# Two residual gates and a norm vector: spread over the partitions by one product with the partial sums, or read broadcast from DRAM

## The chip, the cores and the metric

The kernel runs on one NeuronCore of a Trainium2 chip. The metric is the device time of one execution in microseconds (us). The engines are named as in the profile: PE (TensorE), PEld (its weight loads), DVE (VectorE), ACT (ScalarE), POOL (GpSimd), SP (SyncE, which here only issues DMAs; SPq is its queue).

## The reference, cut to what matters

One layer: a mixing sub-layer (RWKV-7 and a causal convolution, merged by gates) and a squared-ReLU MLP, each added to the residual through a gate that depends on a vector `c`. 512 tokens, 1024 channels, all in float32.

```
mod = silu(c) @ ada_w + ada_b                       # 6 segments of 1024
sh_m, sc_m, gt_m, sh_f, sc_f, gt_f = split(mod, 6)
...
x = x + gt_m * (merged @ w_out)                     # merged: 512 x 2048
h = rms_norm(x, norm_ffn_gain) * (1 + sc_f) + sh_f
x = x + gt_f * (square(relu(h @ w_ff_in)) @ w_ff_out)
return rms_norm(x, final_gain)
```

The change touches `gt_m` (segment 2), `gt_f` (segment 5) and `final_gain`. Each is one value for a channel, and tokens lie on the partitions where they are used, so each must stand in all 128 partitions: a 128x1024 tile.

## The kernel before, in words

Every large product is done in three passes of two fp32r parts: a weight tile `raw` is loaded by DMA, ACT casts it to `hi`, DVE or POOL subtracts to give `lo`, and PE runs hi·high, hi·low, lo·high. The names are `raw_wo`, `hi_wo`, `lo_wo` for the output product and `raw_fi`, `hi_fi`, `lo_fi` for the first MLP product.

The middle of the kernel is a list of steps, written out by hand in `ORDER`: R, I, V, O, M, S, Y are the RWKV part, U and T the convolution, G and B the merging gates (`ga`, `gb`), L reloads merged tiles that were spilled (`mr`), W is one step of the output product, A half a segment of `mod`, Q the spread of the first gate. The number behind a colon is a priority offset: the tile framework's scheduler sorts the instructions of each engine by priority and by when their operands are free, so the order in the program text is not the order on the engines. Every engine then works in its own order and waits where an operand is missing. All weight, `ada_w` and reload DMAs stand in one order on SP.

After the last RWKV group `enter_tail` opens the pools of the tail (near 606 us). What runs from there to 735 us:

- **A steps.** `mod_half` loads eight 128x512 tiles `ar` of `ada_w` (256 KB each, three buffers) and sums them on DVE, each weighted by a column of `silu(c)`, in `aacc`: partial sums that still have to be added over the 128 partitions. `mod_cols` does that with four products with a column of ones (`pmv`, 128x1) and adds the bias (`ab`) into `modt`: one value for a channel, channels on the partitions. There are eight A steps, A0 to A7, for segments 2 to 5: 0 and 1 give gate `gt_m` (`modt[0]`), 2 and 3 `sh_f` (`modt[1]`), 4 and 5 `sc_f` (`modt[2]`), 6 and 7 `gt_f` (`modt[3]`). In the list their order is A3, A0, A5, A7, A1, A6, Q, A2, A4.
- **W steps.** The product of `merged` with `w_out`, in two halves of 512 columns, each 16 row tiles, accumulated over all 16 for four token tiles (`acc_wo`, four PSUM buffers). `wo_out` multiplies by the gate (`t_wo`) and adds to the residual `x`. In the second half the last seven row tiles (`WLATE`) are kept back and run token tile by token tile.
- **h2.** After the last row tile, `h2_norm` for each of the four token tiles (square on ACT, a chain of some ten 128x1 operations on DVE in `srow`, then `xn`) and `h2_tile` (PE transposes `ph`, then scale `modt[2]` and shift `modt[1]` into `hf` on ACT and DVE, and the parts `hh`, `hl`). The first four column tiles of the MLP (`ps_fi`, `ff_part`) run on token tiles 0 and 1 first (128x256 moving), then on 2 and 3.

`spread` is how a gate gets to all partitions: DVE makes a diagonal matrix `dg` from a column of `modt`, PE multiplies ones by it (128x128, float32, two records each), eight times for one gate, and ACT copies 512 columns out of PSUM twice. It runs three times: for `gate_t` in step Q, and for `gate_f` and `fgain` in the MLP, both after its fifth column tile.

Of the kernel before, what the change touches and what calls it, by code (L numbers as in the profile page):

```python
# [8 lines left out]
F32 = mybir.dt.float32  # L9
# [3 lines left out]
ALU = mybir.AluOpType  # L13
# [28 lines left out]
)  # L42
WLATE = 9
# [19 lines left out]
def tile_rwkv7_conformer(  # L63
# [19 lines left out]
    ident = const.tile([P, P], F32, name="ident")  # L83
# [79 lines left out]
    def mm3(ps, w, m):  # L163

        for k in range(KT):
            last = mm3k(ps, w, m, k)
        return last
# [55 lines left out]
            PE.matmul(pm[:, i:i + 1], acc[:, i * P:(i + 1) * P], ones[:, 0:1], start=True, stop=True)  # L223
        V.tensor_tensor(dst[:, 4 * h:4 * h + 4], pm, ab[:, 8 * seg + 4 * h:8 * seg + 4 * h + 4], op=ALU.add)

    def spread(pool, psp, tag, dst, col, nm):

        for h in range(2):
            pb = psp.tile([P, 512], F32, tag=tag, name=f"psp_{nm}{h}")
            for i in range(4):  # L230
                dg = pool.tile([P, P], F32, tag="dg", name=f"dg_{nm}{h}{i}", bufs=2)
                V.tensor_scalar(dg, ident, col[:, 4 * h + i:4 * h + i + 1], None, op0=ALU.mult)
                PE.matmul(pb[:, i * P:(i + 1) * P], ones, dg, start=True, stop=True)
            S.copy(dst[:, 512 * h:512 * h + 512], pb)

    def wrow(src, r0, h, nm, eng=None, own=None):
        raw = wp.tile([P, 512], F32, tag="wraw", name=f"raw_{nm}")
# [9 lines left out]
    with tc.tile_pool(name="e1", bufs=1) as e1, tc.tile_pool(name="e2", bufs=2) as e2:  # L247
# [184 lines left out]
        for n, ap, k in [(n, ap, 8) for n, ap in (  # L432
                ("a0", a0[0]), ("k_k", k_k[0]), ("k_a", k_a[0]), ("r_k", rk_flat), ("gn_gain", gn_gain[0]),
                ("gn_bias", gn_bias[0]), ("conv_b", conv_b[0]), ("ln_gain", conv_ln_gain[0]),
                ("ln_bias", conv_ln_bias[0]), ("nfg", norm_ffn_gain[0]), ("fgain", final_gain))] + [("mu", mu_shift[0], 26)]:
            nc.sync.dma_start(out=rows[1][r:r + k, :], in_=ap.rearrange("(t p) -> t p", p=P))
            VEC[n] = vt[:, r:r + k]
            r += k
        nc.sync.dma_start(out=rows[2], in_=cwr[72:200])
        nc.sync.dma_start(out=rows[3][0:48, :], in_=cwr[200:248])  # L440
        for i, (dst, n0) in enumerate(((vt, 114), (cw[:, 72:200], 128), (cw[:, 200:248], 48))):
            pt = pq.tile([P, 512], F32, tag="m", name=f"ptv{i}", bufs=2)
            PE.transpose(pt[:, 0:n0], rows[i + 1][0:n0, :], ident[0:n0, 0:n0])
            V.tensor_copy(dst, pt[:, 0:n0])
# [8 lines left out]
    with ExitStack() as c1:  # L453
# [368 lines left out]
        def enter_tail():  # L822

            cq.close()
            m2 = c1.enter_context(tc.tile_pool(name="m2", bufs=1, reuse_waits="tile"))
            p2 = ctx.enter_context(tc.tile_pool(name="p2", bufs=1, space=PSUM, reuse_waits="tile"))
            tail["ct"] = c1.enter_context(ExitStack())
            tpool[0] = tail["ct"].enter_context(tc.tile_pool(name="t2", bufs=1, reuse_waits="tile"))
            tail["m2"], tail["p2"] = m2, p2
            tail["mh"], tail["ml"] = {}, {}  # L830
            x1.extend(tok_halves("x1_"))
            gate.append(m2.tile([P, D], F32, tag="gt", name="gate_t"))
            for i in range(2):
                nc.sync.dma_start(out=x1[i], in_=x2d.rearrange("(h t p) n -> h p t n", p=P, t=2)[i])

# [113 lines left out]
        def step(op):  # L949
            k, i = op[0], int(op[1:] or 0)  # L950
            if k == "R":
                quarters.setdefault(i // 2, []).append(rkv_pair(i))
            elif k == "I":
                scans[i] = products(i, quarters[i])
            elif k == "V":
                scans[i] = solve(i, scans[i])
            elif k == "O":
                scans["o", i] = scan_operands(i, quarters[i])
            elif k == "M":
                scans[i] = merge_inverses(i, *scans[i])  # L960
            elif k == "S":
                RT, RVs = scans[i], scans["o", i]
                scans[i] = scan(i, quarters[i], RVs, RT)
            elif k == "Y":
                group_norm(i, quarters[i], *scans[i])
                if i == 3:
                    enter_tail()
            elif k == "U":
                scans["gl", i] = conv_tile(i)
            elif k == "T":  # L970
                conv_taps(i, scans.pop(("gl", i)))
            elif k == "G":
                gate_a(i)
            elif k == "N":
                scans["cn"] = conv_norm()
            elif k == "B":
                gate_b(i, *scans["cn"])
            elif k == "L":
                reload()
            elif k == "A":  # L980
                seg, h = 2 + i // 2, i % 2
                acc = mod_half(modt[seg - 2], seg, h, V)
                mod_cols(pp, "o", modt[seg - 2], acc, seg, h)
            elif k == "Q":
                spread(tail["m2"], tail["p2"], "m", gate[0], modt[0], "gm")
            elif k == "W":
                wo_step(int(wn[0] == 16))

# [5 lines left out]

    p2 = tail["p2"]
    with tc.tile_pool(name="s3", bufs=2, reuse_waits="tile") as s3:
        gate_f = s3.tile([P, D], F32, name="gate_f", bufs=1)
        fgain = s3.tile([P, D], F32, name="fgain", bufs=1)
        ssum = s3.tile([P, NT, 6], F32, name="ssum", bufs=1)

        def ff_rows(acc, n, k, wh, wl, fh, fl, tt):
# [40 lines left out]
        for fq in range(NFQ):  # L1042
            fh = s3.tile([P, KT, T], F32R, tag="fh", name=f"fh{fq}")
            fl = s3.tile([P, KT, T], F32R, tag="fl", name=f"fl{fq}")
            for i in range(KT):
                if fq == 0 and i < NFF:
                    ps = first_ff[i]
                else:
                    w = wcol(w_ff_in[0], fq * D + i * P, f"fi{fq}{i}", G if fq == 0 and GFI > i else None)
                    ps = pp.tile([P, T], F32, tag="pp", name=f"ps_fi{fq}{i}", bufs=2)  # L1050
                    mm_last = mm3(ps, w, (hh, hl))
                f = s3.tile([P, T], F32, tag="f", name=f"f{fq}{i}")
                S.activation(f, ps, AF.Relu)
                V.tensor_tensor(f, f, f, op=ALU.mult)
                S.copy(fh[:, i, :], f)
                V.tensor_tensor(fl[:, i, :], f, fh[:, i, :].bitcast(F32), op=ALU.subtract)
                if fq == 0 and i == max(SPR, NFF):
                    with tc.issue_after(mm_last.ins):
                        spread(s3, p2, "m", gate_f, modt[3], "gf")
                        spread(s3, p2, "m", fgain, VEC["fgain"], "fg")  # L1060
            last = fq == NFQ - 1
            for h in range(2):
                acc = [p2.tile([P, 512], F32, tag="acc", name=f"acc_fo{fq}{h}{tt}", bufs=4) for tt in range(NT)]
                held = []
                for k in range(KT):
                    own = (s3, "late", KT - FLATE) if last and h == 1 and k >= FLATE else None
                    with ahead(LHP if own else 0):
                        wh, wl = wrow(w_ff_out[0], fq * D + P * k, h, f"fo{fq}{h}{k}", None, own)
                    if own:
                        held.append((k, wh, wl))  # L1070
                        continue
                    for tt in range(NT):
                        ff_rows(acc, k, k, wh, wl, fh, fl, tt)
                for tt in range(NT):
                    for k, wh, wl in held:
                        ff_rows(acc, k, k, wh, wl, fh, fl, tt)
                    if last and h == 1:
# [32 lines left out]
```

## Time and profile before

| what | value |
|---|---|
| time, three runs | 1129.80 us median (1123.34 to 1132.21) |
| the profiled execution | 1131.94 us, span 1130.2 us |
| mean granted clock of TensorE | 0.953 of full speed |
| PE busy | 1023.5 us (91%) |
| DVE busy | 790.1 us (70%) |
| ACT busy | 479.1 us (42%) |
| POOL busy | 198.2 us (18%) |
| DMA | 131.34 MB, mean 116 GB/s |

The profile is of one execution; its times start at the first instruction. PE's busy time is modelled at the ends of matmuls, so the distance from one start to the next says more than the duration. "[1.38 <-DVE xn L905]" behind a row means that the engine had been idle 1.38 us and that line 905 on DVE released it.

### The profile page before, as it was taken

How to read it: one execution, taken by the hardware profiler on the slowest of the kernel's cores; microseconds unless marked ns; L12 is line 12 of the kernel's file. 1: busy time of each engine (PE TensorE's matmuls, PEld its weight loads, DVE VectorE, ACT ScalarE, POOL GpSimd, SP SyncE). 2: the span in 40 equal slices, each digit the busy share in tenths (PEclk: the TensorE clock that was granted, in tenths of full speed). 3: DMA queues.
4: the chain of work that ended last, by engine and by line, in shares of the span. 5: the costliest groups of instructions: out<-in, count | busy, mean ns of one | idle time of the engine just before them, and what ended most of it. 6: DMA issues, size and time to landing. Idle time of an engine off the chain costs nothing.

```text
span 1130.2 us, 16757 instructions
## 1 busy us (share of the span) xinstructions
PE 1023.5 (91%) x6037; PEld 792.5 (70%) x6037; DVE 790.1 (70%) x1622; ACT 479.1 (42%) x912; POOL 198.2 (18%) x191
## 2 busy tenths in 40 slices
PE   2999889889899789996997999899999999999995
PEld 1777666656677666665665767688888888888874
DVE  3859999969958997989455787585445445445557
ACT  5546445374644356534343433264323323423432
POOL 1123042222422533221121121200000000000002
PEclk9999999989999989996798999999999999999998
DMA  9622332331343234324257686731223323333332
GB/s 313 181 72 87 88 100 73 54 92 48 104 117 94 86 95 83 85 66 110 94 162 234 224 273 217 232 104 38 84 93 95 101 94 94 95 93 100 96 103 74
DMA packets 184605, 131.34 MB, mean 116 GB/s; under 512 B 49945, under 2 KB 152779, under 8 KB 184523
## 3 DMA queue, kind: packets, MB, share of 16 engines
q1 hardware_dynamic: 184523, 130.28, 39.1%
q8 instruction: 47, 0.77, 0.3%
q14 instruction: 35, 0.29, 0.1%
HBM read 116.61 MB, written 13.63 MB: 115 GB/s over the span
## 4 chain that ended last, share of the span: by engine, by line
PE 43%; DVE 16%; DMA 5%; issue 3%; ACT 3%; POOL 1%; SPq 0%; DVEq 0%; ACTq 0%; POOLq 0%
PE ps_fi L174 5%; PE ps_fi L175 5%; PE ps_fi L176 5%; DVE cz L745 5%; PE acc_fo L1005 4%; PE acc_fo L1004 4%; PE acc_fo L1003 4%; DMA ar<-in_ada_w_dram 2%; DVE tmp L598 1%; DVE aacc L217 1%; PE ps_ga L175 1%; PE ps_ga L176 1%; PE ps_ga L174 1%; DVE X L600 1%; PE pr L669 1%
## 5 line engine op out<-in xcount | busy, mean ns | idle before, releaser
L745 DVE SCALAR_TENSOR_TENSOR cz<-gl,cw,cz 128x512 f32<-128x512 f32 x240 | 200.8, 837 | 3.9 <-ACT cz L743 1.2
L151 DVE TENSOR_TENSOR lo_fo<-raw_fo,hi_fo 128x512 fp32r<-128x512 f32 x64 | 44.2, 691 | 92.1 <-ACT hi_fo L150 91.9
L175 PE MATMUL ps_fi<-hl,hi_fi 128*128 128x512 f32 (+1 forms) x288 | 105.6, 367 | 0.0
L176 PE MATMUL ps_fi<-hh,lo_fi 128*128 128x512 f32 (+1 forms) x288 | 105.3, 367 | 0.0
L174 PE MATMUL ps_fi<-hh,hi_fi 128*128 128x512 f32 (+1 forms) x288 | 105.0, 367 | 0.0
L1003 PE MATMUL acc_fo<-hi_fo,fh 128*128 128x512 f32 x256 | 101.3, 396 | 0.8 <-DVE t_fo L1010 0.8
L1004 PE MATMUL acc_fo<-lo_fo,fh 128*128 128x512 f32 x256 | 101.2, 395 | 0.0
L1005 PE MATMUL acc_fo<-hi_fo,fl 128*128 128x512 f32 x256 | 101.2, 395 | 0.0
L150 ACT CAST hi_fo<-raw_fo 128x512 fp32r<-128x512 f32 x64 | 39.7, 621 | 110.6 <-PE acc_fo L1005 87.8
L151 DVE TENSOR_TENSOR lo_fi<-raw_fi,hi_fi 128x512 fp32r<-128x512 f32 x64 | 43.8, 690 | 52.1 <-ACT hi_fi L150 51.2
L150 ACT CAST hi_fi<-raw_fi 128x512 fp32r<-128x512 f32 x64 | 39.9, 623 | 74.0 <-PE ps_fi L175 45.6
L1021 POOL TENSOR_TENSOR x<-x,fgain 128x512 f32<-128x512 f32 x4 | 5.5, 1392 | 363.8 <-ACT sq L1015 363.8
L175 PEld LDWEIGHTS ps_fi<-hl,hi_fi 128*128 128x128 f32 x288 | 54.3, 189 | 8.9 <-DVE hl L928 0.4
L176 PEld LDWEIGHTS ps_fi<-hh,lo_fi 128*128 128x128 f32 x288 | 54.3, 189 | 8.7
L174 PEld LDWEIGHTS ps_fi<-hh,hi_fi 128*128 128x128 f32 x288 | 54.0, 189 | 8.8 <-ACT hh L927 0.2
L174 PE MATMUL ps_u<-hh,hi_u 128*128 128x512 f32 x128 | 54.1, 422 | 5.4 <-DVE tr L466 2.9
L937 PE MATMUL acc_wo<-lo_wo,mh 128*128 128x512 f32 x128 | 53.0, 414 | 5.9 <-DVE lo_wo L151 3.2
L217 DVE SCALAR_TENSOR_TENSOR aacc<-ar,cact,aacc 128x512 f32<-128x512 f32 x56 | 49.9, 891 | 11.3 <-DMA ar<-in_ada_w_dram 10.7
L1003 PEld LDWEIGHTS acc_fo<-hi_fo,fh 128*128 128x128 f32 x256 | 48.2, 188 | 12.7 <-DVE t_fo L1010 1.3
L1005 PEld LDWEIGHTS acc_fo<-hi_fo,fl 128*128 128x128 f32 x256 | 48.2, 188 | 11.5
L1004 PEld LDWEIGHTS acc_fo<-lo_fo,fh 128*128 128x128 f32 x256 | 48.2, 188 | 11.5
L176 PE MATMUL ps_u<-hh,lo_u 128*128 128x512 f32 x128 | 54.9, 429 | 0.6 <-POOL Pt L512 0.6
(334 smaller groups left out, 2554.3 us busy)
## 6 DMA issues: line engine op xcount, KB each, us to landing
ar<-in_ada_w_dram SPq DMA_DIRECT2D x64, 256.0 KB
raw_fi<-in_w_ff_in_dram SPq DMA_DIRECT2D x64, 256.0 KB
raw_fo<-in_w_ff_out_dram SPq DMA_DIRECT2D x64, 256.0 KB
araw<-in_ada_w_dram SPq DMA_DIRECT2D x8, 1024.0 KB
raw_u<-in_w_in_dram SPq DMA_DIRECT2D x32, 256.0 KB
raw_wo<-in_w_out_dram SPq DMA_DIRECT2D x32, 256.0 KB
raw_k<-in_w_in_dram SPq DMA_DIRECT2D x16, 256.0 KB
raw_v<-in_w_in_dram SPq DMA_DIRECT2D x16, 256.0 KB
```

The costliest lines, as they stand in the source:

```text
L150: S.copy(hi, raw)
L151: (eng or V).tensor_tensor(lo, raw, hi.bitcast(F32), op=ALU.subtract)
L174: PE.matmul(ps[:, ts_], wh[:, i, :], mh[:, k, ts_], start=first, stop=False, skip_group_check=True)
L175: PE.matmul(ps[:, ts_], wh[:, i, :], ml[:, k, ts_], start=False, stop=False, skip_group_check=True)
L176: return PE.matmul(ps[:, ts_], wl[:, i, :], mh[:, k, ts_], start=False, stop=(k == KT - 1), skip_group_check=True)
L217: eng.scalar_tensor_tensor(acc, a, cact[:, k:k + 1], acc, op0=ALU.mult, op1=ALU.add)
L598: V.tensor_tensor(tv, X[:, 0:n, s:s + 1].to_broadcast([P, n, m]), U[:, s:s + 1, s + 1:32].to_broadcast([P, n, m]), op=ALU.mult)
L745: V.scalar_tensor_tensor(cz, gl[:, w:w + T], cw[:, w * KT + j:w * KT + j + 1], cz, op0=ALU.mult, op1=ALU.add)
L937: PE.matmul(wacc[h][tt], mh[k][:, ts_], wl, start=False, stop=False)
L1003: PE.matmul(acc[tt], fh[:, k, ts_], wh, start=(n == 0), stop=False)
L1004: PE.matmul(acc[tt], fh[:, k, ts_], wl, start=False, stop=False)
L1005: PE.matmul(acc[tt], fl[:, k, ts_], wh, start=False, stop=(n == KT - 1))
```

## The change

For segments 2 and 5, `mod_cols` is replaced by `gate_half`: one product of a 128x128 matrix of ones with the 128x512 partial sums puts their sum over the partitions into every partition of a PSUM tile (`pgt`), and one DVE operation adds it to `gate_t` or `gate_f`. Those tiles hold the bias by then: `enter_tail` loads them from `ada_b` with a DMA that reads one row for every partition (512 KB written each). `fgain` is loaded in the same way as the MLP's pool opens. `spread`, its three uses and step Q go. `gate_f` moves from the MLP's pool to one of its own, opened at `enter_tail`.

```diff
-    "L:2000 A5:2000 W:500v W:0v A7:200 A1:1000 W:200 W:1000 W:200v W:100 A6 L:100 W:0v Q:500 W:500 "
+    "L:2000 A5:2000 W:500v W:0v A7:200 A1:1000 W:200 W:1000 W:200v W:100 A6 L:100 W:0v W:500 "
...
-    def spread(pool, psp, tag, dst, col, nm):
-
-        for h in range(2):
-            pb = psp.tile([P, 512], F32, tag=tag, name=f"psp_{nm}{h}")
-            for i in range(4):
-                dg = pool.tile([P, P], F32, tag="dg", name=f"dg_{nm}{h}{i}", bufs=2)
-                V.tensor_scalar(dg, ident, col[:, 4 * h + i:4 * h + i + 1], None, op0=ALU.mult)
-                PE.matmul(pb[:, i * P:(i + 1) * P], ones, dg, start=True, stop=True)
-            S.copy(dst[:, 512 * h:512 * h + 512], pb)
+    def gate_half(psp, tag, dst, seg, h):
+
+        acc = mod_half(None, seg, h, V)
+        pb = psp.tile([P, 512], F32, tag=tag, name=f"pgt{seg}{h}")
+        PE.matmul(pb, ones, acc, start=True, stop=True)
+        hs = slice(512 * h, 512 * h + 512)
+        V.tensor_tensor(dst[:, hs], pb, dst[:, hs], op=ALU.add)
...
             gate.append(m2.tile([P, D], F32, tag="gt", name="gate_t"))
+            gate.append(ctx.enter_context(tc.tile_pool(name="gp", bufs=1, side="right")).tile([P, D], F32, name="gate_f"))
+            for i, seg in enumerate((2, 5)):
+                nc.sync.dma_start(out=gate[i], in_=row(ada_b[0][seg * D:seg * D + D]).partition_broadcast(P))
...
                 seg, h = 2 + i // 2, i % 2
+                if seg in (2, 5):
+                    gate_half(tail["p2"], "m", gate[seg == 5], seg, h)
+                    return
...
-            elif k == "Q":
-                spread(tail["m2"], tail["p2"], "m", gate[0], modt[0], "gm")
...
-        gate_f = s3.tile([P, D], F32, name="gate_f", bufs=1)
+        gate_f = gate[1]
         fgain = s3.tile([P, D], F32, name="fgain", bufs=1)
+        nc.sync.dma_start(out=fgain, in_=row(final_gain).partition_broadcast(P))
...
-                if fq == 0 and i == max(SPR, NFF):
-                    with tc.issue_after(mm_last.ins):
-                        spread(s3, p2, "m", gate_f, modt[3], "gf")
-                        spread(s3, p2, "m", fgain, VEC["fgain"], "fg")
```

The rest of the diff takes `fgain` out of the loads of vectors (`vt` has 106 columns for 114) and makes three `modt` for four.

The scheduler answers with another order. Up to `enter_tail` the two kernels' orders are the same but for names. Behind it, three places.

On SP at the start of the tail, before (`mgd<-z` is the spill of a merged tile, `wg` a small weight of the gates, `ar` the first load of an A step):

```order
L729 DMA yad_133<-yg_5835 128x512
L757 DMA mgd_113<-z_5728 128x512
L213 DMA ar_6188<-in_ada_w_dram 128x512
L773 DMA wg_5856<-in_w_gate_up_dram 128x128
L213 DMA ar_6191<-in_ada_w_dram 128x512
```

and in the changed kernel, where the second of the new loads waits for earlier DMAs, for PE and for ACT:

```order
L755 DMA mgd_112<-z_5726 128x512
L833 DMA gate_t<-in_ada_b_dram 128x1024
L833 DMA gate_f<-in_ada_b_dram 128x1024
L213 DMA ar_6192<-in_ada_w_dram 128x512
L771 DMA wg_5860<-in_w_gate_up_dram 128x128
L213 DMA ar_6195<-in_ada_w_dram 128x512
```

The two gate loads stand ahead of the first `ar`. On SP at the end of the A and W steps, before (all 64 `ar` loads are out before the first `raw_fi`):

```order
L238 DMA raw_wo_6994<-in_w_out_dram 128x512
L213 DMA ar_6862<-in_ada_w_dram 128x512
L213 DMA ar_6865<-in_ada_w_dram 128x512
L213 DMA ar_6868<-in_ada_w_dram 128x512
L238 DMA raw_wo_7000<-in_w_out_dram 128x512
L238 DMA raw_wo_7006<-in_w_out_dram 128x512
L213 DMA ar_6871<-in_ada_w_dram 128x512
L159 DMA raw_fi_7206<-in_w_ff_in_dram 128x4x128
```

and in the changed kernel:

```order
L236 DMA raw_wo_6970<-in_w_out_dram 128x512
L159 DMA raw_fi_7170<-in_w_ff_in_dram 128x4x128
...
L159 DMA raw_fi_7194<-in_w_ff_in_dram 128x4x128
L213 DMA ar_6823<-in_ada_w_dram 128x512
L159 DMA raw_fi_7200<-in_w_ff_in_dram 128x4x128
L213 DMA ar_6826<-in_ada_w_dram 128x512
L159 DMA raw_fi_7206<-in_w_ff_in_dram 128x4x128
L213 DMA ar_6829<-in_ada_w_dram 128x512
L213 DMA ar_6832<-in_ada_w_dram 128x512
L159 DMA raw_fi_7212<-in_w_ff_in_dram 128x4x128
L213 DMA ar_6835<-in_ada_w_dram 128x512
```

The last five `ar` loads of A4 now stand behind the last `raw_wo` and among the first `raw_fi`. On PE, before, A4's products (`pmv_6874`) stand 53 `acc_wo` matmuls before the last of these, and the transposes `ph` of token tiles 0 and 1 lie between those; `acc_wo_6743` is token tile 1, `acc_wo_6744` tile 2:

```order
L938 MATMUL acc_wo_6743<-hi_wo_7008,ml_6655 128x512
L223 MATMUL pmv_6874<-ones,aacc_6849 128x1 x4
L937 MATMUL acc_wo_6744<-lo_wo_6937,mh_6033 128x512
L938 MATMUL acc_wo_6744<-hi_wo_6936,ml_6034 128x512
L936 MATMUL acc_wo_6744<-hi_wo_6954,mh_6061 128x512
```

In the changed kernel A2's products stand at that place, and the end of the output product reads as follows (`acc_wo_6709` is the last token tile, `pmv_6838` is A4, `ph_7044` to `ph_7119` are token tiles 0 and 1):

```order
L937 MATMUL acc_wo_6709<-hi_wo_6972,mh_6646 128x512
L223 MATMUL pmv_6838<-ones,aacc_6813 128x1
L938 MATMUL acc_wo_6709<-lo_wo_6973,mh_6646 128x512
L223 MATMUL pmv_6838<-ones,aacc_6813 128x1
L939 MATMUL acc_wo_6709<-hi_wo_6972,ml_6647 128x512
L223 MATMUL pmv_6838<-ones,aacc_6813 128x1 x2
L919 MATMUL ph_7044<-ident,xn_7026 128x128 x4
L919 MATMUL ph_7056<-ident,xn_7026 128x128 x4
L919 MATMUL ph_7107<-ident,xn_7089 128x128 x4
L919 MATMUL ph_7119<-ident,xn_7089 128x128 x4
L174 MATMUL ps_fi_7218<-hh,hi_fi_7172 128x256
```

A4's products and all transposes now stand at and behind the last `acc_wo`. On DVE in the changed kernel A4's eight sums begin behind `t_wo` of token tile 1, and `xn` of token tiles 0 and 1 stands behind `t_wo` of the last tile; before, A4's sums stood ahead of all four `t_wo`, and both `xn` ahead of the `t_wo` of the last tile.

## Rows read from the trace of the kernel before

**Rows 1.** First part of the page: busy time, share, instructions.
```profile
PE 1023.5 (91%) x6037; PEld 792.5 (70%) x6037; DVE 790.1 (70%) x1622; ACT 479.1 (42%) x912; POOL 198.2 (18%) x191
```

**Rows 2.** Windows: stretch, length, PE, PEld, DVE, ACT, POOL busy, clock, DMA, GB/s.
```profile
600.00:605.00 5.00, 1.60 (x8) 0.98 (x6) 2.13 (x3) 1.06 (x3) 2.56 (x2) 1.00 0.66 211
605.00:610.00 5.00, 2.50 (x5) 1.49 (x5) 1.27 (x3) 1.05 (x2) 0.00 (x0) 0.50 0.79 254
610.00:615.00 5.00, 4.97 (x10) 3.25 (x11) 3.52 (x6) 0.25 (x1) 0.00 (x0) 0.50 0.88 291
615.00:620.00 5.00, 5.00 (x23) 4.13 (x22) 4.77 (x8) 2.64 (x5) 0.00 (x0) 0.98 0.84 254
...
760.00:765.00 5.00, 3.70 (x31) 3.50 (x30) 3.67 (x10) 1.76 (x3) 0.00 (x0) 1.00 0.62 178
```

**Rows 3.** Waits of SP's DMA queue, 600 to 740: total, times, longest (us).
```profile
SPq L213 <- DVE aacc L217: 33.0, 40, 3.6
```

**Rows 4.** Timeline of SP: first `ar` load, last `raw_wo`, last `ar`.
```profile
606.32 0.34 SPq L757 DMA_DIRECT2D mgd<-z  x1
606.71 0.43 SPq L213 DMA_DIRECT2D ar<-in_ada_w_dram  x1
...
728.16 0.90 SPq L238 DMA_DIRECT2D raw_wo<-in_w_out_dram  x2
730.54 0.33 SPq L213 DMA_DIRECT2D ar<-in_ada_w_dram  x1
```

**Rows 5.** Chain of waits, 590 to 800: one of its pieces.
```profile
726.21 2.81 DMA ar<-in_ada_w_dram
```

**Rows 6.** Timeline of PE, from the last weight of the output product.
```profile
736.38 0.50 PE L937 MATMUL acc_wo<-lo_wo,mh 128*128 128x512 f32 x1 [0.47 <-POOL lo_wo L151]
...
737.87 0.95 PE L223 MATMUL pmv<-ones,aacc 128*128 128x1 f32 x8
...
745.63 1.03 PE L918 MATMUL ph<-ident,xn 128*128 128x128 f32 x8
...
752.56 0.39 PE L938 MATMUL acc_wo<-hi_wo,ml 128*128 128x512 f32 x1
752.79 0.51 PE L174 MATMUL ps_fi<-hh,hi_fi 128*128 128x256 f32 x3
...
765.08 1.06 PE L918 MATMUL ph<-ident,xn 128*128 128x128 f32 x8 [1.38 <-DVE xn L905]
```

**Rows 7.** Timeline of DVE: A4's last sum, token tile 1, `xn`.
```profile
734.14 1.04 DVE L217 SCALAR_TENSOR_TENSOR aacc<-ar,cact,aacc 128x512 f32<-128x512 f32 x1 [1.70 <-DMA ar<-in_ada_w_dram]
...
738.96 0.68 DVE L943 TENSOR_TENSOR t_wo<-acc_wo,gate_t 128x512 f32<-128x512 f32 x1
...
741.81 0.69 DVE L151 TENSOR_TENSOR lo_fi<-raw_fi,hi_fi 128x512 fp32r<-128x512 f32 x1
...
745.52 0.75 DVE L905 TENSOR_SCALAR xn<-x,srow 128x1024 f32<-128x1024 f32 x1
```

**Rows 8.** Timeline of ACT: first `hf` of token tile 0, third `hh`.
```profile
746.26 1.86 ACT L922 ACTIVATE hf<-ph,modt,modt 128x128 f32<-128x128 f32 x5 [1.74 <-DVE xn L905]
...
751.88 0.67 ACT L927 CAST hh<-hf 128x512 fp32r<-128x512 f32 x1
```

**Rows 9.** Windows of 20 us in the MLP, columns as in Rows 2.
```profile
780.00:800.00 20.00, 20.00 (x102) 16.00 (x102) 13.18 (x29) 9.81 (x17) 0.00 (x0) 1.00 0.17 53
800.00:820.00 20.00, 20.00 (x88) 16.25 (x87) 7.43 (x11) 6.58 (x11) 0.00 (x0) 1.00 0.29 92
```

**Rows 10.** One tile's instructions: min/median/max ns, first and last start.
```profile
L233 PE MATMUL psp_gm<-dg_gm,ones x16: 270/275/415, 652.0 to 695.9; 128*128 128x128 f32 x16
L233 PE MATMUL psp_gf<-dg_gf,ones x16: 272/275/377, 785.4 to 790.1; 128*128 128x128 f32 x16
L778 PE MATMUL pg<-sgl,wg x16: 590/592/1220, 235.8 to 656.5; 128*128 128x512 f32 x16
L223 PE MATMUL pmv<-ones,aacc x64: 164/250/271, 623.7 to 738.6; 128*128 128x1 f32 x64
```

More of the change, by code (lines that the diff above doesn't have):

```diff
@@ L106, in tile_rwkv7_conformer @@
     VEC = {}
-    vt = const.tile([P, 114], F32, name="vt")
+    vt = const.tile([P, 106], F32, name="vt")
     ab = const.tile([P, 56], F32, name="ab")
@@ L110, in tile_rwkv7_conformer @@
     modv = const.tile([P, 4, KT], F32, name="modv")
-    modt = [const.tile([P, KT], F32, name=f"modt{i}") for i in range(4)]
+    modt = [const.tile([P, KT], F32, name=f"modt{i}") for i in range(3)]
     om = const.tile([P, 26], F32, name="om")
@@ L434, in tile_rwkv7_conformer @@
                 ("gn_bias", gn_bias[0]), ("conv_b", conv_b[0]), ("ln_gain", conv_ln_gain[0]),
-                ("ln_bias", conv_ln_bias[0]), ("nfg", norm_ffn_gain[0]), ("fgain", final_gain))] + [("mu", mu_shift[0], 26)]:
+                ("ln_bias", conv_ln_bias[0]), ("nfg", norm_ffn_gain[0]))] + [("mu", mu_shift[0], 26)]:
             nc.sync.dma_start(out=rows[1][r:r + k, :], in_=ap.rearrange("(t p) -> t p", p=P))
@@ L440, in tile_rwkv7_conformer @@
         nc.sync.dma_start(out=rows[3][0:48, :], in_=cwr[200:248])
-        for i, (dst, n0) in enumerate(((vt, 114), (cw[:, 72:200], 128), (cw[:, 200:248], 48))):
+        for i, (dst, n0) in enumerate(((vt, 106), (cw[:, 72:200], 128), (cw[:, 200:248], 48))):
             pt = pq.tile([P, 512], F32, tag="m", name=f"ptv{i}", bufs=2)
@@ L1050, in tile_rwkv7_conformer @@
                     ps = pp.tile([P, T], F32, tag="pp", name=f"ps_fi{fq}{i}", bufs=2)
-                    mm_last = mm3(ps, w, (hh, hl))
+                    mm3(ps, w, (hh, hl))
                 f = s3.tile([P, T], F32, tag="f", name=f"f{fq}{i}")
```

## The prediction, on record before the run

> **What bounds the kernel now.** I read the busy shares first [rows 1]: PE is busy 91% of the span, so what counts is where PE is idle or slow, and what PE does beside the three-pass products. The windows come next [rows 2]. Two holes near this change are to be seen: 600 to 610, where PE is busy 1.60 and 2.50 us of 5, and 760 to 765, with 3.70. Between them lies the stage of the A and W steps, in which DMA engines are busy 0.79 to 0.88 of the time: SP issues 64 `ar` loads there, from 606.71 to 730.54 [rows 4], one in 1.93 us, and waits 40 times, 33.0 us in all, for DVE to free an `ar` buffer [rows 3]. So that stage is set by a loop of load, sum, free buffer, next load, with a load of 2.81 us in it [rows 5], and PE follows. From 752.79 on [rows 6] PE is full, and what is added or removed there counts whole.
>
> The place to watch is the end of the output product [rows 6]. The last weight comes at 736.38, A4's `pmv` at 737.87, and from there PE runs `acc_wo` without a hole until 752.56; the first `ps_fi` follows 0.23 us later. Below this, DVE [rows 7] goes from `t_wo` of token tile 1 (738.96) to the second `xn` (745.52), PE transposes at 745.63, ACT starts `hf` at 746.26 and has the third `hh` from 751.88 to 752.55 [rows 8], which the first `ps_fi` of the second token tile reads. All of it is hidden under `acc_wo`, just in time.
>
> **The change, part by part.**
>
> *The h2 chain comes out of its cover.* By the new order A4's products stand at the last `acc_wo`, and `xn` and `ph` behind it. Nothing else on PE covers them. The time of the first `ps_fi` is built up so: token tile 1 is done where it was, 737.87; A2's products take 0.95 in place of A4's [rows 6]; 54 `acc_wo` at 0.23 give 12.4, which is 751.2. A4's sums begin behind `t_wo` and `x` of token tile 1, about 2.3 us after 737.87. They are eight at some 0.75, with six `lo_fi` of 0.69 [rows 7] and one `t_wo` and `x` among them: 6 + 4.1 + 1.4 = 11.5, and the last two loads wait for buffers that the fourth and fifth sums free, each 2.81 or more [rows 5]. That ends 0.5 to 4 us behind 751.2; I take 1.5, since only two loads lie on the path: 752.7. Then DVE has what it had between 738.96 and PE's 745.63, that is `t_wo`, `modt`, `x`, three `lo_fi`, the small operations and `xn`: 6.7 [rows 6, 7]. Then from `ph` to the third `hh`: 745.63 to 752.55, 6.9 [rows 6, 8]. In all 766.3 where it was 752.79: **+13.5**, between 9 (the `lo_fi` come early, ACT has less beside it) and 17 (the loads of A4 are 4 us late).
>
> *The hole of before goes.* PE waited 1.38 us at 765.08 for `xn` of a later token tile [rows 6]. That tile's `xn` now has the whole delay to be made in; but the first `ps_fi` will wait for `hl` here and there: **-0.7** (-1.4 to +1).
>
> *The clock.* After the hole at 601 to 606 the granted clock was 0.50 from 605 to 615, that is the 1.2 GHz level, and 0.98 after it [rows 2]. PE was busy 2.50 + 4.97 us at half speed there, so 3.7 us went. The new hole of some 13 us, with a few transposes in it, is longer. **+4** (0 to 6).
>
> *The two spreads in the MLP go.* The window 780 to 800 holds 102 matmul records, the next 88, both with PE at 20.00 [rows 9]. Of the 102, 32 are `psp_gf` (785.4 to 790.1) and the like of `psp_fg` [rows 10]. The other 70 at 20/88 = 0.227 are 15.9, so the spreads took **-4.1**. They stood on a full PE, so this comes back whole. DVE's diagonals and ACT's copies lay beside it.
>
> *The end of the weights.* Five `ar` loads no longer stand ahead of the last `raw_wo`: at most 5 x 1.93 = 9.7 us earlier [rows 4]. Against it the two gate loads write 1 MB at the tail's start, where the DMA moved 254 GB/s [rows 2]: 4.1 us; and the second of them waits on SP. Its wait includes the spill `mgd<-z`, issued at 606.32, and a DMA took 2.81 [rows 4, 5], so all the loads behind it stand some 2.8 us. Ends: -9.7 and +6.9. The sum of both is -2.8, but with SP's waits for DVE [rows 3] not every load in front counts: **-2**.
>
> The Trainium skill, page "DMA: Bandwidth & Descriptors", section "Anatomy of one DMA — SWDGE (gpsimd) path", fits one DMA by 2.0 us and its bytes at 436 GB/s; no window in the rows shows such a rate, the highest is 291 GB/s [rows 2]. By its rate the two loads would be an estimated 2.4 us of transfer, not 4.1, and the sum 1.7 us lower.
>
> *Step Q and the products of the A steps* lie in the stage that the loads set, and cost or give nothing by themselves: 16 records of `psp_gm` and 32 of `pmv` at about 0.25 go, and four `pgt` come; the nearest row is `pg`, 128x512 in float32, two records of 0.59 each [rows 10]. On PE that would be 3 to 8 us fewer if PE set this stage, which it does not. **0** (-3 to +1). The load of `fgain`, 512 KB, goes at DMA shares of 0.17 to 0.29 [rows 9], and its tile is needed at the very end: 0.
>
> The sum is 13.5 - 0.7 + 4 - 4.1 - 2 = +10.7. On the profiled execution, 1131.94, this gives 1142.6. That execution is 2.1 above the median of the runs, so **1140.5**, 0.9% above 1129.8.
>
> **The rivals.**
>
> *Faster: the weights end early.* Place: the last `lo_wo` on PE, 736.38 now. If the loop of buffers gives the five freed slots in full, and the gate loads fit into the gaps that SP's waits leave, that weight comes 9.7 earlier, not 2. Then A4's own loads are early too, and the hole is shorter and the clock holds better (2, not 4). That is 10.7 - 7.7 - 2 = +1; with the chain at its lower end, 9 for 13.5, it is -3.5. Time 1126 to 1131, taken at 1127.5. For it: SP does wait for buffers, not for bandwidth. Against it: 0.79 to 0.88 of the DMA engines' time is taken [rows 2], and only the order of the loads changes, not their number. It decides if the last `lo_wo` comes before 730. Chance 0.22.
>
> *Slower: SP stands behind the gate load.* Place: the second gate load at 606. All `ar`, `wg`, `gy` and `raw_wo` loads queue behind it, and a loop that waits for a buffer at each step carries a lost microsecond to the end. If the 2.8 us and the 4.1 us are carried whole and the five slots are not given back, the term is +6.9, not -2: 10.7 + 8.9 = +19.6, or 1149.5. It decides if the first `ar` goes later than 609 and the last `lo_wo` comes later than 740. Chance 0.22.
>
> *The gates come for nothing.* If the scheduler's order did not matter at the end, because A4's sums were late for another reason or because PE had other work, only the MLP's 4.1 and the 2 would stay: 1123.7. The order shows no such work. Chance 0.04.
>
> **How the numbers follow.** The forecast has 0.52; its own bounds (9 to 17, 0 to 6) reach from 1134 to 1147. 1% of 1129.8 is 11.3 us, and that is about what a measurement of this kernel can tell from no change; the boundary, 1141.1, lies just above the forecast, so half of its chance falls on each side. Slower by over 1%: 0.52 x 0.46 + 0.22 = 0.46. Faster by over 1%, below 1118.5, needs the last rival or the low end of the first: 0.05. The rest, 0.49, is no change that can be told. The range takes in the early weights down to 1127 and the late ones up to 1151.
>
> **What would show it in the profile of the changed kernel.** The h2 chain: a hole on PE of 10 to 16 us between the last `acc_wo` and the first `ps_fi`, ended by `xn` and then by `hh`. The aacc loop: `pmv` of A4 waiting for `aacc` right at the last `acc_wo`. The clock: a window of 0.50 behind that hole. The MLP: from the first 512-wide `ps_fi` to the end some 4 us less. The weights: the last `lo_wo` at 734, give or take 4. The prediction is wrong if `xn` of the first two token tiles stands under running `acc_wo` after all, or if the last weight moves by more than 5 us to either side.

## The result and the profile after

The change makes the kernel slower by 0.7%: 1135.6 us median of 20 runs (1129.49 to 1140.98) against 1126.94 of 20 runs of the kernel before, ratio 1.0074 with a 95% interval of [1.005, 1.0098]. By that ratio it is +8.3 us (the medians themselves are 8.7 apart); +10.7 were forecast.

The two profiled executions, 1131.94 us before and 1129.87 after, say the opposite at first sight. Up to the tail, where both kernels do the same, the one after happened to be 8.6 us faster: the last spill `mgd<-z` goes out at 606.32 before [rows 4] and at 597.73 after. All times of a stage are therefore compared from that instruction on. From there to the end the trace of before has 523.9 us, that of after 530.5.

The page's busy shares after: PE is busy 16.1 us less than in [rows 1], but only 5.0 of that lie in the tail, from which work was taken. The other 11 lie before the last spill, where the same 3776 matmuls kept PE busy for 515.9 us at a mean granted clock of 0.96, against 527.0 at 0.93 in the trace of before.

```profile
PE 1007.4 (89%) x5965; PEld 776.7 (69%) x5965; DVE 786.6 (70%) x1598; ACT 476.5 (42%) x906; POOL 199.3 (18%) x191
```

The timeline of PE at the end of the output product (start, duration, instruction, idle time ahead of it and what ended that); it answers to [rows 6]:

```profile
728.08 0.95 PE L223 MATMUL pmv<-ones,aacc 128*128 128x1 f32 x8
...
740.60 0.39 PE L937 MATMUL acc_wo<-hi_wo,mh 128*128 128x512 f32 x1
741.83 0.35 PE L223 MATMUL pmv<-ones,aacc 128*128 128x1 f32 x2 [0.85 <-DVE aacc L217]
...
742.50 0.48 PE L939 MATMUL acc_wo<-hi_wo,ml 128*128 128x512 f32 x1
742.82 0.50 PE L223 MATMUL pmv<-ones,aacc 128*128 128x1 f32 x4
749.20 1.94 PE L919 MATMUL ph<-ident,xn 128*128 128x128 f32 x8 [5.88 <-DVE xn L906]
751.98 1.12 PE L919 MATMUL ph<-ident,xn 128*128 128x128 f32 x4 [0.84 <-DVE hf L926]
753.78 1.11 PE L919 MATMUL ph<-ident,xn 128*128 128x128 f32 x4 [0.69 <-DVE hf L926]
756.51 1.22 PE L174 MATMUL ps_fi<-hh,hi_fi 128*128 128x256 f32 x4 [1.61 <-ACT hh L928]
```

A4's `pmv` waits 0.85 us for `aacc` at the very end, the first `ph` waits 5.88 for `xn`, and the first `ps_fi` waits for `hh`. Between the last `acc_wo` (742.50) and the first `ps_fi` (756.51) are 14.0 us; before they followed each other at 0.23. On DVE at the same place, to be held against [rows 7]:

```profile
736.21 0.75 DVE L217 SCALAR_TENSOR_TENSOR aacc<-ar,cact,aacc 128x512 f32<-128x512 f32 x1 [0.17 <-DMA ar<-in_ada_w_dram]
...
738.41 0.75 DVE L217 SCALAR_TENSOR_TENSOR aacc<-ar,cact,aacc 128x512 f32<-128x512 f32 x1 [0.84 <-DMA ar<-in_ada_w_dram]
...
743.01 0.69 DVE L944 TENSOR_TENSOR t_wo<-acc_wo,gate_t 128x512 f32<-128x512 f32 x1 [0.73 <-PE acc_wo L939]
...
748.30 1.41 DVE L906 TENSOR_SCALAR xn<-x,srow 128x1024 f32<-128x1024 f32 x2
```

A4's sums run until shortly before the end, with little waiting for their loads, and both `xn` come 5.3 us behind `t_wo` of the last tile. The windows there (columns as in [rows 2]) show the hole and the clock after it:

```profile
740.00:745.00 5.00, 2.47 (x15) 1.83 (x13) 4.24 (x11) 2.73 (x7) 0.00 (x0) 1.00 0.55 157
745.00:750.00 5.00, 0.80 (x4) 0.83 (x5) 4.71 (x25) 0.70 (x2) 0.00 (x0) 0.54 0.63 174
750.00:755.00 5.00, 3.37 (x14) 2.17 (x12) 2.52 (x10) 4.68 (x13) 0.00 (x0) 0.50 0.25 90
755.00:760.00 5.00, 3.49 (x17) 3.49 (x17) 4.18 (x21) 3.89 (x11) 0.00 (x0) 0.50 0.01 2
760.00:765.00 5.00, 5.00 (x36) 5.00 (x34) 2.90 (x7) 2.90 (x8) 0.00 (x0) 0.75 0.00 0
```

On SP, where [rows 4] had the first `ar` 0.39 us behind the spill, it now goes 2.74 behind it, and the last `ar` 139.3 behind it (736.99), where it was 124.2:

```profile
597.73 0.34 SPq L755 DMA_DIRECT2D mgd<-z  x1
598.11 0.43 SPq L833 DMA_DIRECT2D gate_t<-in_ada_b_dram  x1
600.08 0.33 SPq L833 DMA_DIRECT2D gate_f<-in_ada_b_dram  x1
600.47 0.43 SPq L213 DMA_DIRECT2D ar<-in_ada_w_dram  x1
...
736.99 0.33 SPq L213 DMA_DIRECT2D ar<-in_ada_w_dram  x1
```

And in the MLP, against [rows 9], no window holds spread records any more; the first has 107 records because 256-wide `ps_fi` reach into it:

```profile
780.00:800.00 20.00, 20.00 (x107) 17.25 (x106) 9.93 (x15) 8.07 (x14) 0.00 (x0) 1.00 0.17 53
800.00:820.00 20.00, 20.00 (x88) 16.22 (x87) 7.43 (x11) 6.58 (x11) 0.00 (x0) 1.00 0.31 95
```

What the spreads took is read from the first 512-wide `ps_fi` to the first `acc_fo`, the first matmul of the second MLP product. Before, that is 26.4 us:

```profile
779.93 0.40 PE L174 MATMUL ps_fi<-hh,hi_fi 128*128 128x512 f32 x1
...
806.32 0.39 PE L1003 MATMUL acc_fo<-hi_fo,fh 128*128 128x512 f32 x1
```

and after, 21.8:

```profile
784.09 0.40 PE L174 MATMUL ps_fi<-hh,hi_fi 128*128 128x512 f32 x1
...
805.88 0.39 PE L1006 MATMUL acc_fo<-hi_fo,fh 128*128 128x512 f32 x1
```

### The profile page after: what moved, and what is told of

Its sections match the earlier page's. It is cut to its first block, busy times and chain, and to the rows that moved or that the text cites. A ratio compares the mean times of both kernels' runs of the same rounds, so it can differ in the third digit from the quotient of the medians.

```text
span 1128.2 us, 16581 instructions
## 1 busy us (share of the span) xinstructions
PE 1007.4 (89%) x5965; PEld 776.7 (69%) x5965; DVE 786.6 (70%) x1598; ACT 476.5 (42%) x906; POOL 199.3 (18%) x191
## 4 chain that ended last, share of the span: by engine, by line
PE 49%; DVE 29%; DMA 10%; ACT 5%; issue 4%; SPq 1%; POOL 1%; DVEq 0%; ACTq 0%; POOLq 0%
DVE cz L743 11%; PE ps_fi L174 5%; PE ps_fi L176 5%; PE ps_fi L175 5%; PE acc_fo L1008 4%; PE acc_fo L1007 4%; PE acc_fo L1006 4%; DMA ar<-in_ada_w_dram 3%; DVE tmp L596 2%; DVE X L598 2%; PE pr L667 1%; DVE aacc L217 1%; PE psa L184 1%; DMA mr<-mgd 1%; DMA araw<-in_ada_w_dram 1%
## 5 line engine op out<-in xcount | busy, mean ns | idle before, releaser
L174 PEld LDWEIGHTS ps_fi<-hh,hi_fi 128*128 128x128 f32 x288 | 55.2, 193 | 10.7 <-ACT hh L928 2.0
L1008 PEld LDWEIGHTS acc_fo<-hi_fo,fl 128*128 128x128 f32 x256 | 48.2, 188 | 11.5
L1007 PEld LDWEIGHTS acc_fo<-lo_fo,fh 128*128 128x128 f32 x256 | 48.2, 188 | 11.5
L1006 PEld LDWEIGHTS acc_fo<-hi_fo,fh 128*128 128x128 f32 x256 | 48.2, 188 | 11.5
```

The costliest lines, as they stand in the source:

```text
L174: PE.matmul(ps[:, ts_], wh[:, i, :], mh[:, k, ts_], start=first, stop=False, skip_group_check=True)
L1006: PE.matmul(acc[tt], fh[:, k, ts_], wh, start=(n == 0), stop=False)
L1007: PE.matmul(acc[tt], fh[:, k, ts_], wl, start=False, stop=False)
L1008: PE.matmul(acc[tt], fl[:, k, ts_], wh, start=False, stop=(n == KT - 1))
```

## The experiments

Two explanations were set against each other. **Order:** the loss is the h2 chain that the scheduler's new order takes out of its cover, less the gain in the MLP. **Loads:** the loss is the two broadcast loads, by their 1 MB or by the wait on SP. All kernels were timed in five rounds beside the kernel before (12 executions each, 6 of e3 and 8 of e5; the row "after" has the 20 from above). The table gives, from the start of the last `mgd<-z` on SP, the starts of the last `acc_wo`, the first `ps_fi`, the first 512-wide `ps_fi` and the first `acc_fo` on PE (us, one profiled execution each), and the ratio to before.

| kernel | last acc_wo | first ps_fi | first 512-wide | first acc_fo | ratio, 95% interval |
|---|---|---|---|---|---|
| before | 146.2 | 146.5 | 173.6 | 200.0 | 1 |
| after | 144.8 | 158.8 | 186.4 | 208.2 | 1.0074 [1.0050, 1.0098] |
| e1, loads on POOL's queue | 146.4 | 146.6 | 173.5 | 195.3 | 0.9969 [0.9944, 0.9994] |
| e2, no gate load | 147.3 | 147.5 | 174.7 | 196.5 | 0.9936 [0.9913, 0.9960] |
| e3, before with A4 late | 142.4 | 157.1 | 183.7 | 210.1 | 1.0080 [1.0050, 1.0111] |
| e4, loads on ACT's queue | 147.5 | 161.4 | 187.6 | 209.4 | 1.0062 [1.0035, 1.0090] |
| e5, hole filled, 26 + 18 | 145.2 | 161.3 | 185.8 | 207.6 | 1.0073 [1.0048, 1.0098] |
| e6, bias as a row, POOL | 147.9 | 148.1 | 174.8 | 196.5 | 0.9953 [0.9932, 0.9973] |
| e7, loads in the A steps | 150.4 | 150.6 | 176.4 | 198.2 | 0.9989 [0.9964, 1.0013] |
| e8, before, fgain loaded | 146.1 | 146.3 | 173.3 | 197.4 | 0.9986 [0.9970, 1.0002] |
| e9, hole filled, 26 + 8 | 145.2 | 158.7 | 184.3 | 206.1 | 1.0055 [1.0029, 1.0081] |
| e10, A2, A4 ahead of A7, A6 | 150.6 | 159.9 | 187.3 | 209.0 | 1.0036 [1.0007, 1.0064] |
| e11, bias as a row, SP | 146.8 | 147.0 | 172.5 | 194.3 | 0.9949 [0.9920, 0.9977] |

**e1, the same loads on another queue.**

```diff
-                nc.sync.dma_start(out=gate[i], in_=row(ada_b[0][seg * D:seg * D + D]).partition_broadcast(P))
+                nc.gpsimd.dma_start(out=gate[i], in_=row(ada_b[0][seg * D:seg * D + D]).partition_broadcast(P))
```

> The changed kernel with its two gate loads issued by POOL, not SP. The same bytes are moved, but the scheduler's order at the end of the output product is again like that of before: A4's products stand 54 acc_wo matmuls ahead of the last one and the transposes lie between these. Order theory: the hole between the last acc_wo and the first ps_fi (14 us in the changed kernel) goes, and what is left is the gain in the MLP, so 1120 to 1123 us, or 0.994 to 0.997 of the kernel before. Load theory (the two gate loads and their 1 MB cost the time): the bytes stay, so 1131 us or more, at least 1.003 of before.

Measured 0.9969: faster than before. The same 1 MB is moved, and the loss is gone. Its timeline of PE has the first `ps_fi` on the heels of the last `acc_wo`, and the short hole of before at a later token tile:

```profile
748.67 0.39 PE L939 MATMUL acc_wo<-hi_wo,ml 128*128 128x512 f32 x1
748.90 0.40 PE L174 MATMUL ps_fi<-hh,hi_fi 128*128 128x256 f32 x2
...
760.96 1.06 PE L919 MATMUL ph<-ident,xn 128*128 128x128 f32 x8 [0.83 <-DVE xn L906]
```

**e2, no load at all** (the bias is left out of both gates).

```diff
-            for i, seg in enumerate((2, 5)):
-                nc.sync.dma_start(out=gate[i], in_=row(ada_b[0][seg * D:seg * D + D]).partition_broadcast(P))
+            for i in range(2):
+                G.memset(gate[i], 0.0)
```

> As the first, but the gates are set to zero by POOL and not loaded, so that the bias ada_b is left out of both gates. The instruction order is that of the first run. Order theory: within 2 us of the first run, since the loads lie in gaps. Load theory: 4 to 7 us under the first run.

Measured 0.9936, which is 0.0033 under e1: 3.7 us, between what the two explanations said, and the intervals overlap. In the traces e2 is not earlier than e1 at any of the four places. So a price of the loads of up to some 4 us in this place is neither shown nor excluded.

**e3, the loss without the change.** A4 moves behind five W steps ("four" in the expectation is a miscount).

```diff
-    "W:1000v W:1000v W:500v A2 W A4 W:1000v W:200 W:0v W W:100v W:200 W:200v W:2000 W:0v W:100 W W:200 "
+    "W:1000v W:1000v W:500v A2 W W:1000v W:200 W:0v W W:100v A4 W:200 W:200v W:2000 W:0v W:100 W W:200 "
```

> The kernel before, with nothing of the change but step A4 four places later in ORDER. Its products then stand behind the last acc_wo, as in the changed kernel, with no gate load and all three spreads in place. Order theory: slower by the exposed chain alone, 10 to 14 us, so 1137 to 1141 us or 1.009 to 1.012 of before. Load theory: no change beyond 3 us.

Measured 1.0080, or +9 us, just under the 1.009 to 1.012 of the order theory and far from the 3 us of the other. The kernel has no gate load, all spreads, and the same hole as the changed one. Its timeline of PE:

```profile
750.20 0.39 PE L938 MATMUL acc_wo<-hi_wo,ml 128*128 128x512 f32 x1
750.42 0.95 PE L223 MATMUL pmv<-ones,aacc 128*128 128x1 f32 x8
757.53 1.94 PE L918 MATMUL ph<-ident,xn 128*128 128x128 f32 x8 [6.16 <-DVE srow L136]
...
764.85 1.22 PE L174 MATMUL ps_fi<-hh,hi_fi 128*128 128x256 f32 x4 [1.61 <-ACT hh L927]
```

From the last `acc_wo` to the first `ps_fi` are 14.65 us, where the changed kernel has 14.0. A4's last sum on DVE lies far ahead of that:

```profile
738.29 0.74 DVE L217 SCALAR_TENSOR_TENSOR aacc<-ar,cact,aacc 128x512 f32<-128x512 f32 x1
```

It ends 11 us before the last `acc_wo`. So late loads and sums of A4 are not needed for the hole: it is enough that A4's products, `xn` and `ph` stand behind the end of the output product.

**e4, the loads on ACT's queue.** As e1, with `nc.scalar` for `nc.gpsimd`; here the order at the end stays the bad one.

> The changed kernel with its two gate loads issued by ACT, not SP. SP's first ar load no longer waits behind the second gate load, but the order at the end of the output product stays that of the changed kernel. Order theory: 0 to 2.5 us under the changed kernel, so 1133 to 1136, or 1.005 to 1.008 of before. Load theory with the wait on SP as the cost: back to before or under it, 1122 to 1127.

Measured 1.0062. The first `ar` goes 0.4 us behind the spill, as before, and nothing is won by it: the last `acc_wo` is even later than in the changed kernel. The wait on SP is not the cost.

**e5 and e9, the clock.** In both, matmuls into a PSUM tile that nobody reads fill the hole; they differ in the number behind the transposes (18 and 8). The main part of the edit of e5:

```diff
+            dmy = pp.tile([P, T], F32, tag="pp", name="dmy", bufs=2)
+
+            def fill(n, ins):
+                for _ in range(n):
+                    with tc.issue_after(ins):
+                        ins = PE.matmul(dmy, tail["mh"][late[-1][1]][:, 0:P], late[-1][2], start=True, stop=True).ins
+
+            fill(26, end)
+            fill(18, tr)
```

(`end` is the last `acc_wo`, `tr` the last transpose of token tile 1; the lines that return them are left out here.)

> The changed kernel with matmuls that nobody reads in the hole on PE: 26 of 128x512 behind the last acc_wo and 18 behind the transposes of token tiles 0 and 1, about 0.23 us each. They keep TensorE busy but take the place of no work. If the granted clock falls because of the hole, it stays at 1.00 there, and the transposes and the first ps_fi run at full speed: 3 to 4 us under the changed kernel, so 1.004 to 1.005 of the kernel before (1131 to 1132). If the clock costs nothing beside the chain, no change: 1.007.

Measured 1.0073, no change; but the filler got into the way. Its timeline of PE:

```profile
761.89 4.37 PE L893 MATMUL dmy<-hi_wo,mh 128*128 128x512 f32 x18
766.09 1.03 PE L929 MATMUL ph<-ident,xn 128*128 128x128 f32 x8
```

The filler ends near 766, and the transposes of token tile 2 were sorted ahead of the first `ps_fi`, which so came 2.6 us later than in the changed kernel. From there to the first 512-wide `ps_fi` it took 24.4 us for 27.6; 0.8 of these 3.2 us are the eight transposes of token tile 2, which in the changed kernel lie in this part. Gain and loss nearly cancel, and e9 has the shorter filler.

> As the run with matmuls that nobody reads, but 8 in place of 18 behind the transposes, so that they end before the third hh is there and the first ps_fi is not held up. The first ps_fi should start 158.5 to 159 us behind the last spill of a merged tile, as in the changed kernel, and the part from there to the first 512-wide ps_fi take 24.5 us and not 27.6. Clock as a cost: 3 us under the changed kernel, 1.004 to 1.005 of before. No cost: 1.007.

Measured 1.0055. Timeline of PE and one window of e9:

```profile
752.47 1.03 PE L929 MATMUL ph<-ident,xn 128*128 128x128 f32 x8
...
756.98 2.09 PE L893 MATMUL dmy<-hi_wo,mh 128*128 128x512 f32 x8
759.30 0.74 PE L174 MATMUL ps_fi<-hh,hi_fi 128*128 128x256 f32 x4 [0.23 <-ACT hh L938]
```

```profile
755.00:760.00 5.00, 3.62 (x20) 2.52 (x18) 4.30 (x20) 4.99 (x14) 0.00 (x0) 1.00 0.01 5
```

The granted clock stays at 1.00. The first `ps_fi` starts where it did (158.7 for 158.8), after a last `acc_wo` that came 0.4 later: from `ph` to `ps_fi` are 6.8 us for 7.3, so most of this way is ACT's and not PE's (ACT is busy 4.99 of the 5 us). The next part takes 25.6 us for 27.6. The ratio is 0.0019 under that of the changed kernel, 2.1 us, as much as the trace shows (2.0 at the first 512-wide `ps_fi`). The intervals overlap, so the size rests on the trace.

**e6, the bias as one row.** This kernel leaves nothing out.

```diff
-                nc.sync.dma_start(out=gate[i], in_=row(ada_b[0][seg * D:seg * D + D]).partition_broadcast(P))
+                nc.gpsimd.dma_start(out=gate[i][0:1, :], in_=row(ada_b[0][seg * D:seg * D + D]))
...
-        PE.matmul(pb, ones, acc, start=True, stop=True)
         hs = slice(512 * h, 512 * h + 512)
-        V.tensor_tensor(dst[:, hs], pb, dst[:, hs], op=ALU.add)
+        PE.matmul(pb, ones[0:1, :], dst[0:1, hs], start=True, stop=False)
+        PE.matmul(pb, ones, acc, start=False, stop=True)
+        S.copy(dst[:, hs], pb)
```

> The changed kernel with the bias as one row (4 KB loaded into partition 0 of the gate's tile, by POOL's queue) that a second product of ones, one row deep, adds in PSUM; ACT copies the sum out. Nothing is left out. The order at the end of the output product is as in the kernel before. Order theory: as the run without gate loads, 0.992 to 0.995 of before (1118 to 1122). If the loads of 1 MB were nothing and the gain of that run was the left-out work, then as the run with POOL's queue, 0.997.

Measured 0.9953, between both values given; it does not settle what the broadcast costs.

**e11, the same with the rows loaded by SP** where the changed kernel has its loads (`nc.sync` for `nc.gpsimd`).

> As the run with the bias in one row, but the two row loads of 4 KB are issued by SP at the start of the tail, where the changed kernel has its broadcast loads. The order at the end is again one with the transposes between the acc_wo matmuls. It adds to that run the wait on SP alone: the first ar goes 2 to 3 us later than there. If SP's loop of A steps carries that to the end: 0.996 to 0.998 of before. If the slack in the stage takes it: 0.995, as in that run.

Measured 0.9949, as e6. The first `ar` goes 2.5 us behind the spill, and yet the last `acc_wo` is 1.1 earlier than in e6. The interval reaches over the other value, 0.996 to 0.998, as well, so that the slack takes the wait rests on the trace. There, too, something else differs: the granted clock at the start of the tail was back at 1.00 earlier than in e6 (4.5 us behind the spill for 8.1). With e4 this is the second sign that the wait on SP costs nothing in sum.

**e7, the gate loads inside the A steps.**

```diff
         acc = mod_half(None, seg, h, V)
+        if (seg, h) in ((2, 0), (5, 1)):
+            nc.sync.dma_start(out=dst, in_=row(ada_b[0][seg * D:seg * D + D]).partition_broadcast(P))
```

(and the loads in `enter_tail` go)

> The changed kernel with the gate loads still on SP, but each issued inside its first A step and not at the start of the tail. The order at the end of the output product is again that of before, with A4's products 67 matmuls ahead of the last acc_wo. Order theory: 0.995 to 0.998 of before. Load theory: 1 MB on SP's queue is carried by the loop of A steps, 1.002 or more.

Measured 0.9989, worse than the order theory said and better than the other. Timeline of SP:

```profile
603.48 0.33 SPq L230 DMA_DIRECT2D gate_f<-in_ada_b_dram  x1
...
629.17 0.43 SPq L230 DMA_DIRECT2D gate_t<-in_ada_b_dram  x1
```

The chain is covered, but the last `acc_wo` is at 150.4, 4.0 us later than in e1. One load goes in the middle of the stage here. That the bytes are paid for there is likely, but the order of the weights is another one as well, and the runs do not part the two.

**e8, one spread of the MLP alone.**

```diff
+        nc.sync.dma_start(out=fgain, in_=row(final_gain).partition_broadcast(P))
...
-                        spread(s3, p2, "m", fgain, VEC["fgain"], "fg")
```

> The kernel before with fgain loaded by a broadcast DMA and its spread left away; both gates as before, the order of everything else the same. One of the two spreads in the MLP: 2 us under before, 0.998 (0.997 to 0.999). A rival says that the load in the MLP collides with the weight loads: 1.000 or more.

Measured 0.9986, 1.6 us, near the value given, but the interval just reaches 1; the size rests on the trace. From the first 512-wide `ps_fi` to the first `acc_fo` are 24.15 us for 26.38. One spread costs 2.2, two 4.6 (21.79 in the changed kernel).

**e10, the same loads with another list.**

```diff
-    "L:2000 A5:2000 W:500v W:0v A7:200 A1:1000 W:200 W:1000 W:200v W:100 A6 L:100 W:0v W:500 "
-    "W:1000v W:1000v W:500v A2 W A4 W:1000v W:200 W:0v W W:100v W:200 W:200v W:2000 W:0v W:100 W W:200 "
+    "L:2000 A5:2000 W:500v W:0v A2:200 A1:1000 W:200 W:1000 W:200v W:100 A4 L:100 W:0v W:500 "
+    "W:1000v W:1000v W:500v A7 W A6 W:1000v W:200 W:0v W W:100v W:200 W:200v W:2000 W:0v W:100 W W:200 "
```

> The changed kernel with its gate loads as they are, but in ORDER steps A2 and A4 (shift and scale) change places with A7 and A6 (the second gate, which nothing needs before the MLP). A4's products then stand 146 acc_wo matmuls before the last and both xn ahead of the last t_wo, but the scheduler leaves the transposes behind the last acc_wo. Order theory: half of the chain is covered, the hole shrinks from 14 to some 7 us, 5 to 8 us under the changed kernel: 1.000 to 1.003 of before. Load theory: 1.006 to 1.009 as in the changed kernel.

Measured 1.0036, 4 us under the changed kernel and short of what was expected. The hole shrinks from 14.0 to 9.3 us, but the last `acc_wo` comes 5.9 us later, so the first `ps_fi` of this execution is not earlier at all. Timeline of PE:

```profile
749.16 1.02 PE L230 MATMUL pgt<-aacc,ones 128*128 128x512 f32 x2
757.37 1.06 PE L919 MATMUL ph<-ident,xn 128*128 128x128 f32 x8 [1.02 <-DVE srow L136]
...
765.23 1.01 PE L174 MATMUL ps_fi<-hh,hi_fi 128*128 128x256 f32 x3 [3.06 <-ACT hh L928]
```

`ph` hardly waits now, and the rest of the hole is ACT's way from `ph` to `hh`. This trace is of the slowest of the twelve executions (1138.55; the median is 1132.76), and in it the granted clock fell a second time behind the start of the tail: it was 0.50 from 615 to 620, 10 to 15 us behind the spill, where the changed kernel has 1.00. So where its weights end is no measure for the other executions; part of the delay stands at the first `raw_wo` already, which goes out 24.1 us behind the spill for 21.9. The 4 us of the ratio are not explained by the trace, and the run tells the two explanations apart only weakly.

## Why the prediction was right, point by point

*The h2 chain.* Forecast: the first `ps_fi` 13.5 later by the chain, 2 earlier by the weights, so +11.5. Measured 158.8 for 146.5, +12.3. Its pieces: token tile 1 was done 1.2 earlier (130.35 for 131.55; forecast 2). From A2's `pmv` to the last `acc_wo` 14.4 (forecast 0.95 + 12.4 + 1.5 = 14.9). From the last `acc_wo` to `ph` 6.7 (forecast 6.7). From `ph` to the first `ps_fi` 7.3 (forecast 6.9). That this chain is the cause is shown from both sides: e3 makes the loss without the change, e1, e6 and e11 keep the change and lose the loss. One piece mattered less than the prediction had it: A4's late sums held PE up by 0.85 us, and in e3 the hole is there with these sums long done. What counts is the order of A4's products, `xn` and `ph`.

*The clock* was sized too large: +4, where e9 shows 2.0 between the first `ps_fi` and the first 512-wide one, and e5 3.2, or 2.4 without the transposes that ran ahead there. (Another 0.5 lies between `ph` and the first `ps_fi`; it is counted in the 7.3 of the chain.) PE had little to do at half speed, as ACT set the pace from `ph` to `hh`: it was busy 4.68 of the 5 us from 750 to 755. Behind that, the 256-wide `ps_fi` from 756.5 to 762.4 paid. *The hole of before* at 765 was sized too small: -0.7, where that part took 25.6 with the clock kept (e9) and 27.1 before, so -1.5. Together +0.4 (27.6 for 27.1), forecast +3.3. These 2.9 us are the difference between +10.7 and the measured +8.3; what the other terms missed nearly cancels.

*The two spreads in the MLP:* forecast -4.1, measured 21.8 for 26.4, so -4.6; e8 gives half of that for one of them.

*The end of the weights* was -2. The last `lo_wo` was used 2.1 earlier (127.95 behind the spill for 130.06), token tile 1 was done 1.2 earlier, since PE had more of it left to run behind that `lo_wo`. How much of this is the order of the `ar` loads is not shown: at the start of the tail the granted clock was back at 1.00 after 4.4 us, in the trace of before after 8.9. The prediction took a DMA share of 0.79 to 0.88 for the whole stage from windows of its first 15 us; from 620 to 720 the trace of before has 0.63 to 0.84 in windows of 20 us. *Step Q and the A steps* at nothing: no run speaks against it, none measures it alone.

The sum to the first `acc_fo` is 12.3 + 0.4 - 4.6, to the rounding the +8.2 of the table (208.2 for 200.0), and the timed +8.3 agrees. Behind it, the trace of before has another 1.6 us that no other kernel's has (323.9 for 322.3; e3 and e8, which are unchanged there, 322.8 and 322.5), so it is of that execution. The absolute time was forecast 4.9 too high; 2.9 of that lie in the base, for which three runs had given 1129.8 and twenty gave 1126.94. Two sums of the prediction are slightly off: its bounds added up give 1132 to 1146, not 1134 to 1147, and the slower rival comes to 1149.4. And it took 1% as what a measurement can tell from no change; with twenty runs of each kernel 0.74% was told from none.

*The rivals.* "Faster: the weights end early" is out: the weights were 1.2 early, not 9.7. "Slower: SP stands behind the gate load" is out as a cost: the first `ar` was 2.35 us later, as that rival wanted, but the last `lo_wo` was earlier and not later, and e4 and e11 show no cost of that wait. "The gates come for nothing" was right about the gain and wrong about the order: e1 is what it describes.

*What stays open:* whether the 1 MB of broadcast costs anything at the start of the tail (e1 against e2, e6 and e11: 0 to 4 us), and why the weights end later in e7 and e10. That the loads cost nothing in the bad order is not shown either: of the kernels with the hole, e3 without a gate load has its last `acc_wo` earliest (142.4, against 144.8 to 150.6), but it differs from them in more than the loads.

e2 aside, which leaves the bias out, e6 and e11 have the lowest ratios, 0.995 of the kernel before, with the new gates and the old cover; their intervals overlap that of e1.

## What to carry to other kernels

Where a scheduler sorts the instructions, an edit's price is first what it does to the order around a stage's end: here removing work and adding two loads moved a step by 53 matmuls and cost 12 us, and the gain of the edit itself was under 5. Read the order of the changed kernel at the places where one stage hands over to the next, and look for a short chain on other engines that had been hidden by matmuls and now stands behind them. If the chain has come out, try moving the new instructions to another queue or place before giving up the edit; e1 took one word. It has to be tried and its order read: e4 took one word as well, kept the bad order and won nothing clear of noise.

## What the runs showed of the hardware that was not expected

Up to the last spill all these kernels run the same instructions, but for the row of `fgain` and, in e1, e2, e4 and e6, the first gate load or its stand-in, and yet the spill goes out between 597.7 and 607.8 us in the twelve traces after that of before, which has 606.3. The granted clock goes with it: its mean up to the spill is 0.96 in the earliest (after, 597.7), 0.94 in the latest (e3, 607.8) and 0.93 in before. Two windows of before, then of after (columns as in [rows 2]):

```profile
200.00:300.00 100.00, 90.41 (x780) 65.99 (x778) 86.44 (x197) 54.83 (x112) 29.52 (x28) 0.95 0.29 71
500.00:595.00 95.00, 84.78 (x705) 60.88 (x701) 63.02 (x177) 40.02 (x91) 14.17 (x11) 0.82 0.39 114
```

```profile
200.00:300.00 100.00, 86.34 (x776) 62.79 (x776) 88.33 (x204) 57.60 (x114) 30.77 (x29) 1.00 0.30 75
500.00:595.00 95.00, 82.33 (x688) 59.56 (x684) 61.04 (x168) 41.22 (x92) 18.59 (x14) 0.89 0.46 135
```

So one profiled execution differs from another by as much as this change is worth, and only times from a common instruction can be compared. Behind the spill the clock differs once more: it fell to 0.50 around the spill in all thirteen traces and was back at 1.00 between 3.7 and 5.0 us behind it in the five kernels whose new loads stand on SP at the start of the tail (after, e5, e9, e10, e11), between 7.4 and 10.8 in the others. Why is not shown. Matmuls that nobody reads held the clock at 1.00 through a hole of 14 us (e9, e5), where it fell to 0.50 without them.
